# Moving the store of split weight operands from SyncE's queue to ScalarE's

## The chip, the cores and the metric

The kernel runs on one core of a Trainium2 chip. The metric is the device time of one execution in microseconds (us); several executions are given by their median. The engines are PE (TensorE, matmul), DVE (VectorE), ACT (ScalarE), POOL (GpSimd) and SP (SyncE, which here only issues DMAs). An instruction that issues a DMA waits in its engine's own program, in order, for the data and the buffers that it needs; "SPq" in the rows is such an issue on SP.

## What is computed

One layer of a residual trunk on x of 2048 tokens × 1024 channels, float32, cut to what matters (d_ff is 2816, the norms are RMS norms with gains, all mixers are causal):

```python
h = rmsnorm(x, norm_mix_g)
u_lru, u_gate, u_pool = split(h @ w_in)                # 512 columns each
xc = causal_depthwise_conv(u_lru, conv_w, conv_b)      # width 4
y_lru = rg_lru(xc, ...) * gelu(u_gate)                 # gated linear recurrence over the tokens
y_pool = pool_mixer(u_pool, ...)                       # trailing means of 2, 4, 8, 16, minus u
y = concat(rmsnorm(y_lru), rmsnorm(y_pool))
x = x + y @ w_out
h = rmsnorm(x, norm_ffn_g)
x = x + (silu(h @ ffn_w1) * (h @ ffn_w3)) @ ffn_w2
return rmsnorm(x, final_norm_g)
```

## The kernel before

Every large matmul is done on pairs: an operand is split into hi (rounded, written by an ACT copy) and lo (the rest, a subtraction on DVE or POOL), and `mm3` (L237 to L239) multiplies hi·hi, hi·lo and lo·hi into one bank of PSUM. A weight tile `w_hl` holds hi and lo of 128 × 512 weights, 512 KB; there are four such buffers (`wsp`), and six buffers of 256 KB for raw weights as they come from memory (`load_raw`, L208).

A weight is split once, at its first use. `split_kept` writes hi (L224) and lo (L234), and then stores the pair to a cache in device memory (L203). Later uses reload the finished pair from the cache with `kept` (L190, L194) and need no ACT or DVE work. There are 268 stores: 40 go to `cio_d`, the caches of the input and output projections, and 228 to `c13_d` and `c2_d`, those of the feed-forward weights.

The time falls into three stretches. From 0 to about 540 us four chunks of 512 tokens go through norm, input projection (`x_stage`, `u_stage`), the two mixers (`mixers`) and the output projection (`out_stage`); chunk 0 splits the weights, the others reload them. From 540 to 1265 us the feed-forward runs over the first half of the tokens in eleven inner steps, with a Strassen-like scheme of seven products for each block, and splits and stores its weights. From 1265 us on it runs over the second half, out of the cache, without a store of this kind.

The order of the instructions on each engine isn't written out: a scheduler sets it from a simulated timeline and from priorities (`AHEAD` 400 and `FIRST` 1500 for splits, evacuations and norms). So a change of one line can move other instructions, on other engines too.

In the mixer of chunk 0 (`mixers`), names in the order listings are: `ps_g` the gate products, `t0` and `t1` the gates' tanh (L431), `th` and `t0` again the tanh and exponential of the decay (L439, L440), `m` the input factor (L445 to L447, with a square root on ACT), the product of `t1` and `m` on POOL (L453), the scan `xc` (L455), `win` the pooling windows on POOL (L470), `pl` the pooled values (L474), and `sq` the squares (L288, L291) for the norm, whose column sums are small matmuls (L256). `x_hi` and `x_lo` (L337, L338) are the pair of the next chunk's input. In the feed-forward `f_hi`/`f_lo` is the pair of an activation, `e` and `u` are evacuations from PSUM.

Of the kernel before, what the change touches and what calls it, by code (L numbers as in the profile page):

```python
# [9 lines left out]
F32 = mybir.dt.float32  # L10
# [60 lines left out]
def trunk(ctx: ExitStack, tc: tile.TileContext, xT, w_io, w13, w2, gates, pool_w, w_inT, vecs,  # L71
          consts, outT):
    nc = tc.nc
# [103 lines left out]
    def wsp(name, shape):  # L177
        return pool.tile(list(shape), F32R, name=name, tag="wsp", bufs=N_WSP)
# [19 lines left out]
    def split_kept(src, cache, prepare=AHEAD, eng=None):  # L198

        w_ = wsp("w_hl", (P, 2, W))  # L200
        with tc.high_priority(prepare):
            split(w_[:, 0], w_[:, 1], src, eng)
        nc.sync.dma_start(cache, w_.bitcast(F32))  # L203
        return w_[:, 0], w_[:, 1]

    def load_raw(src, shape):
# [24 lines left out]
    def split(hi, lo, src, eng=None):  # L231

        copy_a(hi, src)
        (eng or nc.vector).tensor_tensor(lo, src, hi.bitcast(F32), ALU.subtract)  # L234
# [114 lines left out]
    def weights(blk):  # L349

        if blk in split_before:
            return [kept(cio_d[blk, h]) for h in range(2)]
        split_before.add(blk)
        src = wp_d[blk - 8] if 8 <= blk < 12 else w_io[blk if blk < 8 else blk - 4]
        raw = [load_raw(src[:, NB * h:NB * (h + 1)], (P, NB, P)) for h in range(2)]
        return [split_kept(raw[h].rearrange("p k m -> p (k m)"), cio_d[blk, h], FIRST, eng("w", blk))
                for h in range(2)]
# [226 lines left out]
    def ffn1(hf, j, w, ops, s, after):  # L584
# [14 lines left out]
        def product(n, ps, a, b, fresh):  # L599
            wh, wl = split_kept(b, c13_d[j, w, n]) if hf == 0 else kept(c13_d[j, w, n])  # L600
            for kk in range(NB):
                col = slice(kk * P, kk * P + P)
                mm3(ps, wh[:, col], wl[:, col], a[0][:, kk], a[1][:, kk],
                    fresh and kk == 0, kk == NB - 1, skip_group_check=True)
# [76 lines left out]
    def ffn2(hf, j, s, acc, G):  # L681
# [15 lines left out]
        def product(n, banks, a, b, fresh):  # L697
            wh, wl = split_kept(b, c2_d[j, n]) if hf == 0 else kept(c2_d[j, n])
            for dp, ps in enumerate(banks):
                col = slice(P * dp, P * (dp + 1))  # L700
                mm3(ps, wh[:, col], wl[:, col], a[0], a[1], fresh, True, skip_group_check=True)
# [260 lines left out]
```

## Time and profile before

| | before |
|---|---|
| median of 3 executions | 1935.81 us (1935.36 to 1936.9) |
| profiled execution | 1939.97 us |
| its span | 1938.2 us |
| PE busy | 1832.8 us, 95% |
| DVE busy | 1355.5 us, 70% |
| POOL busy | 928.5 us, 48% |
| ACT busy | 769.5 us, 40% |
| mean granted clock of PE | 0.977 |

The span is the profiled part of that one execution. An engine's busy time leaves out the issuing of DMAs. All views of the trace are of this one execution; the time of a change is measured against the median.

### The profile page before, as it was taken

The numbers are of one execution on the slowest core, as the hardware profiler recorded it, in microseconds if no ns is written. First come the engines' busy times: TensorE is split into PE (matmuls) and PEld (weight loads), VectorE is DVE, ScalarE is ACT, GpSimd is POOL, SyncE is SP. The second block draws the span as 40 slices with busy tenths as digits, with TensorE's granted clock in tenths as the row PEclk, the third lists the DMA queues.
The fourth block names the chain that finished last, engine by engine and source line by source line (L and its number), as shares of the span: only waits on it lengthen the run. The fifth ranks groups of instructions, "written<-read, shape, count | busy, mean of one in ns | idle before, by whom it ended". The sixth has DMA issues, their size and how long they took to land.

```text
span 1938.2 us, 23419 instructions
## 1 busy us (share of the span) xinstructions
PE 1832.8 (95%) x8016; PEld 1487.6 (77%) x8016; DVE 1355.5 (70%) x2004; ACT 769.5 (40%) x1294; POOL 928.5 (48%) x633
## 2 busy tenths in 40 slices
PE   7989999999988999999999999799999999999996
PEld 5778888787767777777777787577888888888885
DVE  7598499876669778777887878875444445444457
ACT  5463546362334444443444434442322223322223
POOL 3361723332136567666676668373333334432373
PEclk9999999999989999999999999899999999999998
DMA  9956855476987666566656666868555555555552
GB/s 322 321 206 219 323 201 179 148 288 227 394 328 260 227 246 223 217 238 220 245 210 231 230 246 230 313 206 298 186 197 194 195 187 183 201 190 195 195 174 87
DMA packets 160838, 444.69 MB, mean 229 GB/s; under 512 B 17872, under 2 KB 20048, under 8 KB 155728
## 3 DMA queue, kind: packets, MB, share of 16 engines
q1 hardware_dynamic: 160720, 443.20, 64.1%
q8 instruction: 63, 1.03, 0.2%
q14 instruction: 55, 0.45, 0.1%
HBM read 275.36 MB, written 167.77 MB: 229 GB/s over the span
## 4 chain that ended last, share of the span: by engine, by line
PE 69%; DVE 17%; issue 5%; DMA 3%; ACT 2%; POOL 2%; SPq 0%; DVEq 0%; ACTq 0%; POOLq 0%
PE ps L239 17%; PE ps L237 16%; PE ps L238 16%; DVE w_hl L234 3%; PE pV L238 2%; PE pV L239 2%; PE pV L237 2%; PE pX L237 2%; PE pX L238 2%; PE pX L239 2%; DMA c_d<-w_hl 1%; PE pY L237 1%; PE pY L238 1%; PE pY L239 1%; DVE sf L719 1%
## 5 line engine op out<-in xcount | busy, mean ns | idle before, releaser
L710 POOL TENSOR_TENSOR G<-G,e 128x512 f32<-128x512 f32 x152 | 227.8, 1516 | 132.1 <-ACT e L224 129.7
L239 PE MATMUL ps<-h_hi,w_hl 128*128 128x512 f32 x616 | 249.0, 405 | 26.2 <-DVE w_hl L234 26.0
L237 PE MATMUL ps<-h_hi,w_hl 128*128 128x512 f32 x616 | 245.5, 401 | 17.7 <-DVE u L636 10.2
L238 PE MATMUL ps<-h_lo,w_hl 128*128 128x512 f32 x616 | 244.9, 398 | 0.0
L237 PE MATMUL ps<-h_hi,w_kept 128*128 128x512 f32 x616 | 240.9, 392 | 2.0 <-DMA w_kept<-c_d 1.2
L238 PE MATMUL ps<-h_lo,w_kept 128*128 128x512 f32 x616 | 240.9, 391 | 0.0
L239 PE MATMUL ps<-h_hi,w_kept 128*128 128x512 f32 x616 | 238.8, 391 | 0.0
L291 POOL TENSOR_TENSOR sq<-sq 128x512 f32<-128x512 f32 (+1 forms) x71 | 99.7, 1407 | 167.0 <-ACT sq L288 165.6
L239 PEld LDWEIGHTS ps<-h_hi,w_hl 128*128 128x128 f32 x616 | 117.9, 191 | 65.7 <-DVE w_hl L234 40.9
L234 DVE TENSOR_TENSOR f_lo<-sf,f_hi 128x512 fp32r<-128x512 f32 x80 | 92.3, 1154 | 106.8 <-PE pZ L238 37.9
L237 PEld LDWEIGHTS ps<-h_hi,w_hl 128*128 128x128 f32 x616 | 118.0, 191 | 49.6 <-ACT w_hl L224 11.2
L710 POOL TENSOR_TENSOR acc<-acc,e 128x512 f32<-128x512 f32 x80 | 123.3, 1570 | 61.5 <-ACT e L224 60.2
L632 POOL TENSOR_TENSOR u<-u,u 128x512 f32<-128x512 f32 x44 | 66.1, 1502 | 179.2 <-DVE u L630 179.1
L706 DVE TENSOR_TENSOR acc<-pV,acc 128x512 f32<-128x512 f32 x160 | 107.9, 685 | 47.4 <-PE pV L239 46.6
L234 DVE TENSOR_TENSOR w_hl<-raw,w_hl 128x512 fp32r<-128x512 f32 x120 | 130.7, 1091 | 12.1 <-ACT w_hl L224 11.6
L238 PEld LDWEIGHTS ps<-h_lo,w_hl 128*128 128x128 f32 x616 | 118.1, 192 | 25.2
L237 PEld LDWEIGHTS ps<-h_hi,w_kept 128*128 128x128 f32 x616 | 115.8, 188 | 27.8 <-DVE acc L837 1.6
L239 PEld LDWEIGHTS ps<-h_hi,w_kept 128*128 128x128 f32 x616 | 115.7, 188 | 25.4 <-DMA w_kept<-c_d 0.3
L238 PEld LDWEIGHTS ps<-h_lo,w_kept 128*128 128x128 f32 x616 | 115.8, 188 | 25.0
L224 ACT ACTIVATE f_hi<-sf 128x512 fp32r<-128x512 f32 x80 | 50.6, 633 | 202.3 <-DVE sf L719 151.9
L224 ACT ACTIVATE w_hl<-t 128x512 fp32r<-128x512 f32 x96 | 60.3, 628 | 165.6 <-DMA c_d<-w_hl 83.2
L237 PE MATMUL ps<-x_hi,w_kept 128*128 128x512 f32 x288 | 115.0, 401 | 1.4 <-DVE u_g L388 1.4
(359 smaller groups left out, 4520.1 us busy)
## 6 DMA issues: line engine op xcount, KB each, us to landing
c_d<-w_hl SPq DMA_DIRECT2D x228, 512.0 KB, 2.9
w_kept<-c_d SPq DMA_DIRECT2D x130, 512.0 KB, 3.7
w_kept<-c_d SPq DMA_DIRECT2D x196, 256.0 KB, 3.4
w_kept<-cio_d SPq DMA_DIRECT2D x68, 512.0 KB, 3.9
raw<-w SPq DMA_DIRECT2D x132, 256.0 KB, 3.3
w_kept<-cio_d SPq DMA_DIRECT2D x104, 256.0 KB, 3.3
cio_d<-w_hl SPq DMA_DIRECT2D x40, 512.0 KB, 5.2
h_lo<-h_d SPq DMA_DIRECT2D x14, 1024.0 KB, 9.6
```

The source lines that it names most:

```text
L224: return nc.scalar.activation(out, in_, AF.Copy)
L234: (eng or nc.vector).tensor_tensor(lo, src, hi.bitcast(F32), ALU.subtract)
L237: i = nc.tensor.matmul(ps, wh, xh, start=first, stop=False, **kw)
L238: nc.tensor.matmul(ps, wh, xl, start=False, stop=False, **kw)
L239: nc.tensor.matmul(ps, wl, xh, start=False, stop=last, **kw)
L291: eng.tensor_tensor(total, total, sq, ALU.add)
L632: nc.gpsimd.tensor_tensor(u3, u3, u2, ALU.add)
L706: nc.vector.tensor_tensor(dst[dp], ps, dst[dp], ALU.add)
L710: nc.gpsimd.tensor_tensor(dst[dp], dst[dp], e, ALU.add)
L719: nc.vector.tensor_tensor(out, a, b, op)
```

## The change

The store of a split pair is issued by ACT (`nc.scalar`) where it was issued by SP (`nc.sync`). All loads, and all other stores, stay on SP.

```diff
--- before.py
+++ after.py
@@ -200,7 +200,7 @@
         w_ = wsp("w_hl", (P, 2, W))
         with tc.high_priority(prepare):
             split(w_[:, 0], w_[:, 1], src, eng)
-        nc.sync.dma_start(cache, w_.bitcast(F32))
+        nc.scalar.dma_start(cache, w_.bitcast(F32))
         return w_[:, 0], w_[:, 1]
```

Three places of the new order follow. A row has the line, the operation, out<-in, the tile's size and how many alike follow each other.

SP at the start of the program, before and then after: `x_raw` is the input of chunk 0, `raw` a raw weight, `cio_d_75<-w_hl` the store.

```order
L325 DMA x_raw_174<-xT 128x512 x3
L325 DMA x_raw_192<-xT 128x512 x3
L203 DMA cio_d_75<-w_hl_180 128x1024
L203 DMA cio_d_75<-w_hl_184 128x1024
L325 DMA x_raw_192<-xT 128x512
L208 DMA raw_302<-w_io 128x512
```

```order
L325 DMA x_raw_174<-xT 128x512 x3
L325 DMA x_raw_192<-xT 128x512 x4
L208 DMA raw_302<-w_io 128x512
L208 DMA raw_304<-w_io 128x512
L208 DMA raw_340<-w_io 128x512
```

The fourth load of x_raw_192 and the weight loads behind it stood behind two stores and now stand ahead of every store.

ACT where the mixer of chunk 0 meets the input of chunk 1, before and then after.

```order
L224 ACTIVATE w_hl_802<-raw_796 128x512
L479 ACTIVATE y_p_1058<-pl_1071,bs_70,vec_60 128x512
L337 ACTIVATE x_hi_840<-x_raw_836,vec_60 128x512 x4
L337 ACTIVATE x_hi_850<-x_raw_838,vec_60 128x512 x4
L431 ACTIVATE t0_918<-ps_g_964,hb_67 128x512
L431 ACTIVATE t1_919<-ps_g_969,hb_67 128x512
```

```order
L224 ACTIVATE w_hl_802<-raw_796 128x512
L203 DMA cio_d_75<-w_hl_798 128x1024
L479 ACTIVATE y_p_1058<-pl_1071,bs_70,vec_60 128x512
L203 DMA cio_d_75<-w_hl_802 128x1024
L431 ACTIVATE t0_918<-ps_g_964,hb_67 128x512
L431 ACTIVATE t1_919<-ps_g_969,hb_67 128x512
L439 ACTIVATE th_1002<-t0_918,sp2_170 128x512
L440 ACTIVATE t0_918<-t0_918,nsp4_172 128x512
L337 ACTIVATE x_hi_840<-x_raw_836,vec_60 128x512 x4
L337 ACTIVATE x_hi_850<-x_raw_838,vec_60 128x512 x4
```

The first gates' tanh and exponential stood behind the eight x_hi copies and now stand ahead of them. DVE in the same mixer, before and then after:

```order
L452 SCALAR_TENSOR_TENSOR t1_919<-t1_919,xc_917 128x512
L441 SCALAR_TENSOR_TENSOR t0_918<-t0_918,th_1002 128x512
L474 SCALAR_TENSOR_TENSOR pl_1097<-win_1095,u_p3_831 128x512
L477 TENSOR_TENSOR first_1099<-win_1095,cst_62 128x16
L478 TENSOR_TENSOR pl_1097<-first_1099,u_p3_831 128x16
L445 SCALAR_TENSOR_TENSOR m_1010<-t0_918 128x512
```

```order
L445 SCALAR_TENSOR_TENSOR m_1010<-t0_918 128x512
L452 SCALAR_TENSOR_TENSOR t1_919<-t1_919,xc_917 128x512
L446 TENSOR_SCALAR m_1010<-m_1010 128x512
L451 TENSOR_SCALAR t0_918<-t0_918 128x512
L441 SCALAR_TENSOR_TENSOR t0_918<-t0_918,th_1006 128x512
L474 SCALAR_TENSOR_TENSOR pl_1097<-win_1095,u_p3_831 128x512
```

The factor m_1010 stood behind the pooled values pl_1097 and now stands ahead of them; the first L452 and the L441 of th_1002 have moved further ahead, before the x_lo of the next chunk.

ACT in one step of the feed-forward, before and then after.

```order
L224 ACTIVATE w_hl_8564<-t3_8562 128x512
L224 ACTIVATE w_hl_8590<-raw_8524 128x512
L224 ACTIVATE e_8490<-pY_8458 128x512
L224 ACTIVATE e_8493<-pY_8459 128x512
L224 ACTIVATE w_hl_8620<-raw_8618 128x512
L224 ACTIVATE f_hi_8638<-s_8309 128x512
```

```order
L224 ACTIVATE w_hl_8590<-raw_8524 128x512
L203 DMA c13_d_76<-w_hl_8564 128x1024
L224 ACTIVATE e_8490<-pY_8458 128x512
L224 ACTIVATE e_8493<-pY_8459 128x512
L203 DMA c2_d_77<-w_hl_8590 128x1024
L224 ACTIVATE w_hl_8620<-raw_8618 128x512
L224 ACTIVATE f_hi_8638<-s_8309 128x512
```

The copies keep their order, and a store now stands between the evacuations e and the hi copy of the next weight, w_hl_8620.

## Rows read from the trace of the kernel before

**Rows 1.** The page, busy time of an engine.

```profile
PE 1832.8 (95%) x8016; PEld 1487.6 (77%) x8016; DVE 1355.5 (70%) x2004; ACT 769.5 (40%) x1294; POOL 928.5 (48%) x633
```

**Rows 2.** Windows: length, busy us and instructions per engine, clock, DMA share, GB/s.

```profile
0.00:100.00 100.00, 86.26 (x392) 69.93 (x393) 62.74 (x150) 52.47 (x85) 35.18 (x31) 0.97 0.91 324
...
600.00:1200.00 600.00, 571.69 (x2429) 454.63 (x2428) 491.22 (x571) 263.69 (x469) 415.69 (x261) 0.99 0.63 230
...
1300.00:1850.00 550.00, 546.90 (x2392) 449.03 (x2392) 269.30 (x362) 151.57 (x257) 196.29 (x142) 1.00 0.59 204
```

**Rows 3.** The line of the store: ns min/median/max, first and last start.

```profile
L203 SPq DMA_DIRECT2D c_d<-w_hl x228: 319/320/1511, 546.3 to 1262.6; - x114
L203 SPq DMA_DIRECT2D cio_d<-w_hl x40: 319/327/1342, 8.1 to 221.2; - x40
```

**Rows 4.** Waits of SP's queue: us in total, times, longest.

```profile
SPq L203 <- DVE w_hl L234: 455.8, 210, 6.9
```

**Rows 5.** Timeline of SP's queue at the start: start us, us.

```profile
4.01 2.54 SPq L325 DMA_DIRECT2D x_raw<-xT  x4
8.13 1.00 SPq L203 DMA_DIRECT2D cio_d<-w_hl  x2
9.18 0.86 SPq L325 DMA_DIRECT2D x_raw<-xT  x1
```

**Rows 6.** Timeline of ACT at the start, with the wait in brackets.

```profile
17.18 0.72 ACT L337 ACTIVATE x_hi<-x_raw,vec 128x512 fp32r<-128x512 f32 x1 [1.46 <-DMA x_raw<-xT]
```

**Rows 7.** Timeline of PE at the start.

```profile
17.96 0.50 PE L237 MATMUL ps<-x_hi,w_hl 128*128 128x512 f32 x1 [2.50 <-ACT x_hi L337]
```

**Rows 8.** The page, DMA queues: packets, MB, share of 16 engines.

```profile
q1 hardware_dynamic: 160720, 443.20, 64.1%
```

**Rows 9.** The chain that ended last, from 92 to 150 us: start, us.

```profile
98.21 0.73 ACT x_hi L337
...
111.52 5.09 issue
116.64 1.41 POOL t L453
...
141.56 0.43 PE ps L237
...
145.83 0.43 PE ps L238
```

**Rows 10.** Timeline of DVE from 98 to 120 us.

```profile
98.97 2.75 DVE L338 SCALAR_TENSOR_TENSOR x_lo<-x_raw,vec,x_hi 128x512 fp32r<-128x512 f32 x3 [2.27 <-ACT x_hi L337]
...
109.67 0.68 DVE L441 SCALAR_TENSOR_TENSOR t<-t,th 128x512 f32<-128x512 f32 x1
111.55 0.69 DVE L474 SCALAR_TENSOR_TENSOR pl<-win,u_p 128x512 f32<-128x512 f32 x1 [1.20 <-POOL win L470]
...
118.07 2.29 DVE L455 TENSOR_TENSOR_SCAN xc<-t,t 128x512 f32<-128x512 f32 x1 [0.59 <-POOL t L453]
```

**Rows 11.** Timeline of PE from 134 to 150 us.

```profile
139.06 1.86 PE L256 MATMUL cols<-ones,sq 128*128 128x1 f32 x8 [6.89 <-DVE sq L291]
```

**Rows 12.** Waits: us in total, times, longest us.

```profile
ACT w_hl L224 <- DMA c_d<-w_hl: 87.3, 28, 5.1
...
PE ps L239 <- DVE w_hl L234: 26.0, 23, 2.5
```

**Rows 13.** Timeline of all engines in one feed-forward step.

```profile
984.82 0.63 ACT L224 ACTIVATE w_hl<-raw 128x512 fp32r<-128x512 f32 x1
...
985.65 1.78 DVE L234 TENSOR_TENSOR w_hl<-raw,w_hl 128x512 fp32r<-128x512 f32 x1
...
988.93 0.39 PE L237 MATMUL ps<-h_hi,w_hl 128*128 128x512 f32 x1
```

## The prediction

> **What bounds the kernel now.** I read the page first: TensorE (PE) is busy 95% of the span [rows 1], so the end moves only where PE stands still or runs at a lower clock. The windows say where. From 1300 to 1850 us PE never lacks work: 2392 matmuls in 546.90 us, 0.2286 us each. By that pace the 2429 matmuls between 600 and 1200 us need 555 us of 600, so about 45 us are lost there, and the 392 in the first 100 us need 90, so 10 are lost [rows 2]. The changed line stops acting at 1262.6 us [rows 3]: the whole second half has no stores of this kind, and can only be shifted.
>
> Then the stores themselves. There are 268, each holds its queue for 0.32 us in the median and at most 1.51 us [rows 3]: 268 × 0.32 = 86 us of queue time that moves from SP to ACT. What SP does most around them is wait for their data: 455.8 us in 210 waits for the DVE subtraction [rows 4]. A store thus leaves when its lo half exists, and no queue can send it sooner. What leaves sooner is a load that now stands behind such a waiting store.
>
> **The change part by part.**
>
> *The start.* The first order fences show the fourth load of x_raw_192 behind two stores on SP. SP issues x loads until 6.55 us, waits until 8.13 us for store data, spends 1.00 us on the two stores, and starts the load at 9.18 us [rows 5]. The load's arrival ends ACT's wait at 17.18 us [rows 6], and PE's wait of 2.50 us at 17.96 us for the x_hi made from it [rows 7]. In the changed order all four loads stand ahead of everything else, so this one can leave near 6.6 us, 2.6 us earlier. The next weights (raw_302) stand right behind and move by as much, so the next PE operand moves along. I take −2.5 us. Bounds: 0, if the data path is already full (the DMA engines are 0.91 busy over the first 100 us [rows 2]) and only the order of bytes changes; −5, if PE is also spared a stretch at the lower clock like the one priced below.
>
> A rule of the Trainium skill speaks against this gain: DMA: Bandwidth & Descriptors, "Issuing engines are not separate DMA queues", says that transfers run on the same 16 engines and interleave whichever engine started them, and that several issuers save only the initiation time on the sequencer, usually small. By it the time would stay near 1935.8. The trace agrees as to the bandwidth (all of this traffic shows as one queue class, 64.1% of the engines' time [rows 8]); but here SP's wait for the store's data stands ahead of the load as well, and the rule does not count that.
>
> *The mixer of the first chunk.* The schedule moves work here, though no store is on the path. Before, ACT runs eight x_hi copies from 98.21 us, which wait for PE, ahead of the gate tanh t0_918; DVE runs pl_1097, which waits for the fourth pooling window until 111.5 us, ahead of m_1010; so POOL's product t1 starts at 116.64 us, when ACT's square root of m is there, 5.09 us after its last window ended [rows 9, 10]. At the end of this chain PE stands for 6.89 us before the column sums at 139.06 us [rows 11], and the eleven matmuls at 141.56 to 145.83 us run at 0.43 us each rather than 0.23, the lower of the clock's two levels: 11 × 0.2 = 2.2 us [rows 9]. After, tanh stands ahead of x_hi, and m_1010 ahead of pl_1097, so t1 can follow the last window at once. But these 5.09 us are not the gain, since DVE is nearly continuously busy from 98.97 to 139 us and the same work stands ahead of the sum in both orders. What it saves is its idle time: two instructions of 0.68 us (L452, L441) that move into its wait of 2.27 us before 98.97, and the waits of 1.20 and 0.59 us at 111.55 and 118.07 [rows 10]. 1.36 + 1.20 + 0.59 = 3.15; I take −3. Bounds: 0, if other waits fill in, and −5.09 − 2.2 = −7.3.
>
> *The first half of the feed-forward, 540 to 1265 us (228 stores).* Here a raw load that stood behind a store leaves up to one issue, 0.32 us, earlier. It waits for a raw buffer first, which the same lo subtraction frees, so the queue costs it no more than that. PE's stalls are mostly waits for lo halves (26.0 us in 23 waits for DVE's w_hl [rows 12]), made by DVE in order behind other DVE work. On ACT 0.32 us is added per store, while ACT is busy 263.69 of 600 us [rows 2], so the cover is ACT's idle time. But ACT works in order, and a store now holds whatever stands behind it until lo is done. The tightest place I found is in the third pair of order fences: the store of w_hl_8590 stands ahead of the hi copy of w_hl_8620. Its lo ends at 985.65 + 1.78 = 987.43 us; with 0.32 for the issue and 0.63 for the copy, hi is there at 988.38, against 984.82 + 0.63 before. PE first wants it at 988.93 [rows 13]. The margin is 0.55 us, and the next thing late is that matmul. I take 0 for the stretch. Bounds: −3.5 (one 0.32 us in each of eleven steps, reaching PE each time) and +26 (below).
>
> Other reordered work (gates of chunk 1, the turn into the feed-forward) has no stall that I can tie to the move; I take 0, ±3.
>
> The sum: −2.5 − 3 + 0 = −5.5. The profiled execution took 1939.97 us, 1938.2 of it span, and 4.2 more than the median of 1935.81, so the traced stalls may be a little large; I apply the difference to the median: 1930.3 us.
>
> **The rivals.** *No change* (chance 0.27): the loads were bound by buffers and by bandwidth, the start's 2.5 us are lost again to the next operand, and DVE stays full in the mixer. For it: DMA 0.91 busy at the start, DVE's full row. Against it: the 2.50 us wait has one releaser, that load. One of the two gains alone leaves 1933, none 1935.8; the case runs from 1932 to 1939.7. The rule of the Trainium skill cited above (DMA: Bandwidth & Descriptors, same section) puts the result here.
>
> *Slower, ACT held by its own stores* (0.21). Mechanism: in each step of the feed-forward a store holds ACT until a lo half is done, and the hi copy behind it comes after PE wants it. It decides once an issue on ACT costs over 0.32 + 0.55 = 0.87 us, or lo ends that much later in the new order. At SP's longest issue, 1.51 us, the example's hi is at 989.57, 0.64 us late. With two to four such places in each of some ten full steps that is 13 to 26 us: 1943 to 1956. For it: ACT already waits 87.3 us in 28 waits for stores to land before it may overwrite a buffer [rows 12], so a late store returns to ACT as a late buffer. Against it: the typical issue is 0.32 us.
>
> *A larger gain* (0.12, part of faster): both gains reach their bounds with the clock kept high, and loads gain in each step: −5 − 7.3 − 3.5 = −15.8, 1920.
>
> **How the numbers follow.** My forecast, with gains between 4 and 10 us, has 0.40. What a measurement of this kernel can tell from no change is 0.2%, 3.9 us: faster is below 1931.9 (0.40 + 0.12 = 0.52), same up to 1939.7 (0.27), slower above (0.21). The forecast's own range is 1926 to 1932. The range for 8 in 10 goes from 1921, which leaves out the extreme of the larger gain, to 1943, which takes in no change and the slower case up to where its worked prices begin (small misses on ACT, and reorderings at +3, lie between 1939.7 and 1943).
>
> **What would show it.** Right: the fourth load of x_raw_192 issued near 7 us and no wait of 2.5 us on PE near 18 us; t1 on POOL right behind the fourth window, and the wait before the column sums shorter by about 3 us; the same 45 us lost between 600 and 1200 us. Wrong: PE waiting for ACT's w_hl (not DVE's) in every step; stores on ACT lasting near 1 us; or the start's transfers landing no earlier than before.

## The result and the profile after

The changed kernel takes 1958.01 us in the median (1956.21 to 1960.4), the kernel before beside it 1936.36: ratio 1.0113, 95% interval [1.0095, 1.013]. I had forecast 1930.3 us, between 1921 and 1943. It is slower, and 15 us above the upper end of the range. Two of the runs below had one execution each far above the others at a lower granted clock (2264.59 and 3028.12 us); their ratios leave these out, their medians do not.

The windows of the changed kernel, columns as in [rows 2]:

```profile
0.00:100.00 100.00, 88.14 (x411) 70.99 (x412) 68.07 (x156) 59.02 (x94) 34.88 (x31) 1.00 0.91 327
...
600.00:1200.00 600.00, 550.63 (x2333) 437.61 (x2334) 469.33 (x547) 251.38 (x449) 374.86 (x248) 0.99 0.61 220
...
1300.00:1850.00 550.00, 546.42 (x2395) 449.30 (x2394) 275.06 (x371) 149.50 (x254) 202.83 (x147) 0.99 0.60 204
```

Against [rows 2], the first 100 us hold 411 matmuls where they held 392, so the start is ahead. From 600 to 1200 us there are 2333 where there were 2429: 96 × 0.2286 = 22 us lost within this window. From 1300 us on nothing differs. A count of PE's instructions in the trace, from zero, says when the n-th one starts, and makes the place exact:

```
n-th PE instruction   before us   after us   lead
 200                     57.94      55.37    -2.57
 600                    156.84     152.47    -4.37
1400                    332.03     328.99    -3.04
1600                    382.83     374.14    -8.69
2600                    630.69     617.67   -13.01
5400                   1333.02    1349.30   +16.27
8000                   1915.99    1932.23   +16.24
```

In these two executions the stretch up to the feed-forward gained 13 us, more than I had hoped for, and the feed-forward lost 29. Each column is one execution: that of the kernel before took 3.6 us more than the median given here and that of the changed kernel 1.8 less, so a gain in this table can be some us too large and a loss too small. The stores of the feed-forward in the changed kernel, and ACT's waits (us in total, times, longest):

```profile
L203 ACTq DMA_DIRECT2D c_d<-w_hl x228: 326/327/389, 535.9 to 1270.5; - x114
```

```profile
ACT u L224 <- DVE w_hl L234: 41.9, 16, 3.0
...
ACT w_hl L224 <- DVE w_hl L234: 23.8, 23, 1.6
...
ACT e L224 <- DVE w_hl L234: 17.8, 20, 2.7
```

Issuing on ACT costs 0.33 us, as on SP [rows 3]. But ACT now waits 83.5 us in 59 waits for DVE's lo halves, with a store in front of the work named; in the kernel before such a wait shows once, with 2.8 us. That looks like my slower rival, ACT held by its stores. The experiments had to say whether it is.

One step of the feed-forward after the change, PE, then DVE, then POOL, from the timeline (start us, us):

```profile
1045.26 0.50 PE L237 MATMUL ps<-h_hi,w_hl 128*128 128x512 f32 x1 [1.33 <-DVE u L636]
...
1059.25 0.50 PE L239 MATMUL ps<-h_hi,w_hl 128*128 128x512 f32 x1 [2.61 <-DVE w_hl L234]
```

```profile
1044.51 0.69 DVE L636 TENSOR_TENSOR u<-ps,u 128x512 f32<-128x512 f32 x1 [2.42 <-POOL u L632]
```

```profile
1041.62 1.62 POOL L596 TENSOR_TENSOR t__9190<-raw,t 128x512 f32<-128x512 f32 x1
1043.21 1.27 POOL L632 TENSOR_TENSOR u<-u,u 128x512 f32<-128x512 f32 x1
```

PE waits 1.33 us for a sum u3 (L636), which waits for POOL's addition (L632), which stands behind a weight combination t2_ of 1.62 us. Later in the step it waits 2.61 us for a lo half. No store stands in this chain on DVE or POOL: what has changed there is the order. In the program's order, POOL and then DVE, before (-) and after (+):

```
-L632 TENSOR_TENSOR u3_8882<-u3_8882,u2_8858 128x512
 L596 TENSOR_TENSOR t2__9190<-raw_9084,t1_9188 128x512
+L632 TENSOR_TENSOR u3_8882<-u3_8882,u2_8858 128x512

-L670 TENSOR_TENSOR c_8944<-ps_8839,u2_8858 128x512
 L234 TENSOR_TENSOR w_hl_9032<-raw_9030,w_hl_9032 128x512
+L670 TENSOR_TENSOR c_8944<-ps_8839,u2_8858 128x512
 L671 TENSOR_TENSOR s_8743<-s_8743,c_8944 128x512
```

Over the whole run PE's waits for lo halves have grown from 26.0 us [rows 12] and those for this sum from 11.0 us; the first row is of the kernel before, the other two of the changed one:

```profile
PE ps L237 <- DVE u L636: 11.0, 3, 7.9
```

```profile
PE ps L239 <- DVE w_hl L234: 41.1, 35, 2.9
PE ps L237 <- DVE u L636: 21.6, 12, 8.0
```

So three theories stood: **hold** (ACT waits in order for lo halves), **order** (the schedule planned the engines' work anew for the new queue), and **queues** (a second DMA queue, with the issue on ACT).

### The profile page after: what moved, and what is told of

The parts are those of the page before. It is cut to its first block, busy times and chain, and to the rows that moved or that the text cites. A ratio compares the mean times of both kernels' runs of the same rounds, so it can differ in the third digit from the quotient of the medians.

```text
span 1954.4 us, 23367 instructions
## 1 busy us (share of the span) xinstructions
PE 1828.6 (94%) x8016; PEld 1480.6 (76%) x8016; DVE 1357.5 (69%) x2004; ACT 767.5 (39%) x1294; POOL 916.5 (47%) x633
## 4 chain that ended last, share of the span: by engine, by line
PE 60%; DVE 20%; POOL 7%; issue 6%; DMA 4%; ACT 2%; SPq 0%; ACTq 0%; DVEq 0%; POOLq 0%
PE ps L239 15%; PE ps L237 14%; PE ps L238 14%; DVE w_hl L234 4%; DVE f_lo L234 2%; POOL t L596 2%; DMA raw<-w 2%; PE pX L239 1%; PE pX L237 1%; PE pX L238 1%; PE pV L238 1%; PE pV L239 1%; PE pV L237 1%; DVE xc L417 1%; PE pY L237 1%
## 5 line engine op out<-in xcount | busy, mean ns | idle before, releaser
L710 POOL TENSOR_TENSOR G<-G,e 128x512 f32<-128x512 f32 x152 | 223.5, 1488 | 113.8 <-ACT e L224 113.8
L234 DVE TENSOR_TENSOR w_hl<-raw,w_hl 128x512 fp32r<-128x512 f32 x120 | 126.5, 1055 | 30.6 <-ACT w_hl L224 25.1
L632 POOL TENSOR_TENSOR u<-u,u 128x512 f32<-128x512 f32 x44 | 64.0, 1455 | 177.7 <-DVE u L630 177.7
L596 POOL TENSOR_TENSOR t<-raw 128x512 f32<-128x512 f32 x44 | 71.0, 1616 | 107.8 <-DVE w_hl L234 50.1
```

Of the source, the lines that this page charges most:

```text
L596: nc.gpsimd.tensor_tensor(t, a, b, ALU.subtract)
L632: nc.gpsimd.tensor_tensor(u3, u3, u2, ALU.add)
L710: nc.gpsimd.tensor_tensor(dst[dp], dst[dp], e, ALU.add)
```

## The experiments

**Halves of the change.** The store gets its queue as an argument (its default is SP or ACT, and the call for the projections names the other): only the projections' 40 stores on ACT, or only the feed-forward's 228.

```diff
-    def split_kept(src, cache, prepare=AHEAD, eng=None):
+    def split_kept(src, cache, prepare=AHEAD, eng=None, q=nc.sync):
...
-        nc.sync.dma_start(cache, w_.bitcast(F32))
+        q.dma_start(cache, w_.bitcast(F32))
```

> Only the 40 stores of the projection weights (cio_d) go to ACT, the 228 of the feed-forward stay on SP. The changed kernel is 13 us ahead of the kernel before at its 2600th matmul (617.67 against 630.69 us) and 16 us behind at the end, so it lost 29 us in the feed-forward. All theories (ACT held by its stores; POOL's new order; two DMA queues that share the engines) put the loss with the feed-forward's stores. Then the time is 1936 - 11 to - 13 = 1923 to 1925 us. If instead the feed-forward loses because of what comes out of the mixers, it stays near 1950.

> The opposite half: the 228 feed-forward stores on ACT, the 40 projection stores on SP. If gain and loss are separate, the loss stands alone: 1936 + 26 to 29 = 1962 to 1965 us. If the loss is less, say 1950, the two halves act on each other.

Measured 1930.97 us (ratio 0.9966 [0.9952, 0.998]) and 1969.04 us (1.0163 [1.0146, 1.018]). Gain and loss are separate, and each stands with its own stores: 7 us gained, 31 lost. Against the kernel before beside them, 1937.91 us, the gain is 4 us smaller and the loss 2 us larger than the ranges that I had taken from the table of single executions.

**Stores later, and POOL's order.** First each feed-forward store is issued behind the hi copy of the next weight; then, instead, POOL's u3 is kept ahead of t2_; then both. From the edits, against the changed kernel:

```diff
-        nc.scalar.dma_start(cache, w_.bitcast(F32))
+        if eng:
+            nc.scalar.dma_start(cache, w_.bitcast(F32))
+        else:
+            store_pending(hi)
+            pending.append((cache, w_))
```

```diff
+            if name == "t2_" and "u3" in last:
+                issue_after(i, last["u3"])
```

> The feed-forward store of a weight is issued on ACT only after the hi copy of the next weight, so that copy is no longer held by it. POOL's order keeps t2_ ahead of u3 as in the changed kernel, and the number of stores and queues is the same. Theory hold (ACT waits in order for lo halves; 87.5 us of ACT's waits are for DVE's lo halves against 2.8 before): most of the 29 us comes back, 1933 to 1942 us. Theory order (POOL's t2_ ahead of u3 makes PE wait for DVE's u): some 14 us stay, 1945 to 1952 us. Theory queues (loads and stores share the DMA engines and land later): no change, 1955 to 1960 us.

> The change, with POOL's add into u3 made to stand ahead of the next weight combination t2_, as it stood before the change. Stores stay on ACT as in the changed kernel. Theory order: PE's waits for DVE's u (22 us in ten waits against 8 in one) go and 10 to 14 us come back, 1944 to 1948 us. Theory hold: the hi copies are as late as they were, at most a few us come back, 1952 to 1958 us. Theory queues: 1955 to 1960 us.

> Both mends at once: the feed-forward store behind the hi copy of the next weight, and POOL's u3 ahead of t2_. Stores later alone gave 1941.1 us, u3 first alone 1948.4, the change 1958. If hold and order are two separate losses, both go and the time is that of the variant with only the projection stores on ACT, 1929 to 1934 us. If the order only mattered through the hold, it stays near 1941, 1938 to 1943 us.

Measured 1941.13 us (1.002 [1.0006, 1.0035]), 1948.43 us (1.0062 [1.0045, 1.008]) and 1943.96 us (1.0036 [1.0022, 1.0051]). Each mend brings back 10 to 17 us, and they don't add up: with both the time is above either of the ranges I had given. But with each edit the schedule planned everything anew: with both edits DVE's order within a step is again that of the kernel before. So these runs can't tell hold from order, though by what was expected of it the first looked like a proof of hold.

**Holding ACT without a DMA.** Stores stay on SP. In the place that each store has in the changed kernel, ACT reads one column of the lo half; a second version reads 176 columns. The heart of the edit:

```diff
+                    i = nc.scalar.activation(small("touch", 1), waiting.pop(0)[:, 1, 0:1].bitcast(F32),
+                                             AF.Copy)
+                issue_after(i, hi)
```

> All stores back on SP, as in the kernel before. In the place of each of the 228 feed-forward stores ACT runs a copy of one column of the lo half, in the place among the hi copies that the store has in the changed kernel (in 144 of 228 ahead of the next hi copy). So ACT waits for every lo half, and no DMA is issued from ACT. Theory hold: the feed-forward loses 20 to 30 us, 1955 to 1967 us. Theory queues (a second queue of DMAs, issue cost on ACT): within a few us of the kernel before, 1935 to 1941 us.

> As the kernel in which ACT reads one column of every lo half in the place of the store (1935.6 us, no loss), but it reads 176 columns, so that ACT is busy for about as long as with the issue of a store, 0.33 us, rather than 0.20. The queue alone, with the old order, cost 9 us. If that is ACT's issue time, 1941 to 1947 us; if it is what the second queue does to landings, 1934 to 1938 us.

Measured 1935.55 us (0.9992 [0.998, 1.0004]) and 1938.96 us (1.0006 [0.9995, 1.0016]). The waits of the first of them, of ACT and then of PE:

```profile
ACT touch L211 <- DVE w_hl L250: 166.3, 138, 3.2
```

```profile
PE ps L256 <- DVE w_hl L250: 30.3, 29, 2.5
```

ACT was held for 166.3 us, twice as long as in the changed kernel, and PE's wait for lo halves is 30.3 us against 26.0 before [rows 12]. So holding ACT for every lo half is not enough for the loss. The wider read took 0.347 us each, about as long as the issue of a store, and cost nothing either. In both, DVE and POOL ran the feed-forward in the order of the kernel before. The schedule was planned with the reads in it, so this does not say what a hold costs in an order that was not planned for it.

**Order and queue, crossed.** The order in which PE, DVE, ACT and POOL run their instructions is taken from one of the two programs and imposed on the other, by a chain of edges that set the issue order alone.

```diff
+    for steps in ISSUE.values():
+        n, ahead = 0, None
+        for step in steps.split():
+            n += int(step)
+            if ahead:
+                tc.add_manual_dep(nc.get_inst_by_name(f"I-{n}"), ahead, mybir.DependencyInfo(
+                    mybir.DependencyClass.NoSync, mybir.DependencyReason.DATA), reason="issue order")
+            ahead = f"I-{n}"
```

> All stores on SP as before the change, but PE, DVE, ACT and POOL run their 11733 computing instructions in exactly the order that they have in the changed kernel. Holding ACT for every lo half without a DMA cost nothing, so the theory hold has fallen; two are left. Theory order: the loss lies in the order that the schedule planned for the new queue, and comes with it: 1950 to 1962 us. Theory queues (what issuing and landing from ACT's queue does, together with the places of the stores on ACT): the order alone costs little, 1924 to 1938 us.

> All stores on ACT as in the changed kernel, but PE, DVE, ACT and POOL run their computing instructions in exactly the order of the kernel before; a store stands ahead of the next hi copy in 137 of 228 places (144 in the changed kernel). Theory order: no loss in the feed-forward, 1931 to 1940 us. Theory queues: the loss stays though the order is the old one, 1950 to 1968 us. Both in part: between.

Measured 1959.01 us (1.0103 [1.0086, 1.012]) for the new order with the stores on SP, and 1947.87 us (1.005 [1.0033, 1.0066]) for the old order with the stores on ACT. The first is the time of the changed kernel to 1 us, with all stores on SP. Its windows row, ACT's wait and PE's waits:

```profile
600.00:1200.00 600.00, 556.41 (x2317) 441.59 (x2318) 478.79 (x546) 247.78 (x446) 379.69 (x247) 0.97 0.60 219
```

```profile
ACT w_hl L224 <- DVE w_hl L234: 2.9, 1, 2.9
```

```profile
PE ps L239 <- DVE w_hl L234: 37.8, 24, 2.9
...
PE ps L237 <- DVE u L636: 16.5, 9, 8.0
```

ACT waits for a lo half once, 2.9 us, and still 2317 matmuls fit where 2429 did. SP's order was left free, but its loads in the feed-forward stand as before. So the new order alone is enough for a loss of this size. It is not made in quite the same way: of the 600 us PE stands idle for 43.6 here and for 49.4 in the changed kernel, against 28.3 before, and the granted clock is 0.97 here and 0.99 in the other two. In the changed kernel hi copies also come late, as DVE's wait for them says; here it is 48.1 us in 38 waits, before 39.2 in 36:

```profile
DVE w_hl L234 <- ACT w_hl L224: 63.2, 81, 4.5
```

How much of the changed kernel's own loss passes through these late copies was not parted. The second run shows that the queue, or the places of the stores on it, can cost something with the old order: 9 us.

**Which engine's order.** Stores on SP; only POOL's order in the feed-forward is the new one, or only that of DVE and ACT (these two were not parted, and PE's order there was left to the schedule, which planned most of the new one).

> Stores on SP, and the computing order of the kernel before on PE, DVE and ACT; only POOL runs the feed-forward in the order of the changed kernel (t2_ ahead of u3 among others). The whole order cost 20 us with stores on SP. If POOL's part is what makes PE wait for DVE's u, 10 to 14 us, so 1947 to 1953 us; if the loss lies with DVE and ACT, under 5 us, 1934 to 1943 us.

> The other part: stores on SP, POOL in the order of the kernel before, DVE and ACT in the feed-forward in the order of the changed kernel (hi copies of raw weights and of activations ahead of evacuations, lo halves ahead of the sums), PE's order there left to the schedule. If the loss lies here, 12 to 20 us, 1949 to 1958 us; if it lies with POOL, under 5 us, 1934 to 1943 us.

Measured 1944.77 us (1.004 [1.0025, 1.0055]) and 1961.94 us (1.0125 [1.011, 1.014]). POOL's order, where I had looked first, costs 6 us, between the two ranges given; that of DVE and ACT, with the order of PE that was planned for it, costs 23 us, which is 4 above its range. Together they make 29 us, about what the whole order loses in the feed-forward: the 20 us by which it is slower, and the 7 that it gains in the mixers, as the runs on the mixers will show.

**Where the 9 us of the queue are.** Stores on ACT, the old order, and each feed-forward store behind the next hi copy.

> All stores on ACT, computing order of the kernel before on PE, DVE, ACT and POOL, and each feed-forward store behind the hi copy of the next weight. With the stores at their free places this order took 1947.9 us, 9 over the kernel before. ACT's busy time and its waits for lo halves cost nothing with the DMAs on SP. If the 9 us need the store ahead of the next hi copy, 1934 to 1941 us; if they come from what the second queue does to landings wherever the store stands, 1944 to 1950 us.

Measured 1933.6 us (0.9975 [0.9959, 0.9991]): not 9 us slower but 5 faster; where the 5 come from was not followed up. The queue itself is no cost here; a store on it ahead of the next hi copy is. DVE's wait for hi copies tells it, first with the stores at their free places, then with the later ones:

```profile
DVE w_hl L234 <- ACT w_hl L224: 64.6, 76, 4.3
```

```profile
DVE w_hl L247 <- ACT w_hl L237: 43.1, 36, 5.2
```

In the kernel before, this wait is 39.2 us in 36 waits, so with the stores at their free places some 40 more hi copies came late. With the reads of one column in like places it was 44.8 us in 50. Why they did less stays open; their schedule was planned with them, while this order was imposed.

**The gain in the mixers.** Only the first weight block's two stores on ACT; only the other 38; and all on SP with the new order up to the first feed-forward weight.

> Only the two stores of the first weight block go to ACT; the fourth load of x_raw_192 then stands ahead of all stores. If the start is worth the 2.5 us that the wait at 17.96 us showed, PE is 2 to 3 us ahead at its 200th matmul and the time is 1933 to 1936 us by this chip's 1937.9 for the kernel before, less what later reordering takes back.

> The other 38 projection stores go to ACT, the first two stay on SP. If the start gives 2.5 us of the 7 that all 40 gave, the rest gives 4 to 5: 1933 us, with no lead at the 200th matmul and a lead between the 1400th and the 1600th, where the column sums at 367.70 us wait. If the lead at the 1600th matmul hangs on the start, this shows no change, 1936 to 1939 us.

> Stores on SP. Up to the first feed-forward weight the computing order of the changed kernel, from there that of the kernel before. If the lead that the changed kernel has after the mixers is the order's as well (7.5 us with the order alone at the 2200th matmul, 2.2 us with the queue alone), the time is 1929 to 1932 us, as good as with the projection stores on ACT.

Measured 1935.39 us (0.9997 [0.9986, 1.0008]), 1930.88 us (0.9963 [0.995, 0.9976]) and 1931.17 us (0.9965 [0.9952, 0.9978]). The first block's stores alone give nothing in the end, though PE is 2.4 us ahead at its 200th instruction. The second run gave the whole gain of the 40 stores, and against what I had expected PE was 2.3 us ahead at its 200th instruction there too, though the fourth load of x_raw_192 still left behind two stores. The 7 us come with the new order, and also with the stores on SP.

**What the runs point to.** The mixers' new order, the feed-forward's old one, all stores on ACT, those of the feed-forward later.

> What the runs point to, in one kernel: all stores on ACT, each feed-forward store behind the hi copy of the next weight, the changed kernel's computing order up to the first feed-forward weight and the old order from there. The mixers' order gave 7 us with stores on SP, the later stores with the old order 4 to 5. If they add up, 1925 to 1929 us by 1938 for the kernel before; if the lead does not carry over, 1931 to 1934 us.

Measured 1927.91 us (0.994 [0.9926, 0.9953]): 10 us faster than before, 30 faster than the change.

## Why the prediction was wrong

**The step that failed** is the feed-forward's "I take 0 for the stretch", with bounds of −3.5 and +26: it measured +29 in the traces and 31 by the medians of the run with these stores alone. I walked one place of the new order through on ACT, with the times of DVE and POOL as they had been, and put the rest under "Other reordered work ... I take 0, ±3". But DVE's and POOL's orders had changed in every step too, and ACT's in part: the hi copy of a combined weight passed that of an activation. The new orders alone are enough for the loss: 1959.01 us with the stores where they were.

**The slower rival** named the stretch and a price of the right size (13 to 26 us, chance 0.21), and a mechanism that is not the main one; that its times of 1943 to 1956 us lie near the measured one is in good part luck. It was to decide once an issue on ACT cost over 0.87 us, or lo ended that much later in the new order. The issue costs 0.33. Its sign, PE waiting for ACT's w_hl in every step, did not show (11.6 us in 7 waits, 13.4 in 9 before). Lo does come later (41.1 us of PE's waits against 26.0), but it does so with no store on ACT too (37.8). Held for 166.3 us, ACT lost nothing. A store's place ahead of the next hi copy does cost 9 us with the old order; that is the part of the rival that is left.

**The start**, −2.5 us. PE was 2.57 us ahead at its 200th instruction. The x loads now leave in one piece, until 7.37 us, and no wait of 2.5 us is left at 18 us:

```profile
4.02 3.35 SPq L325 DMA_DIRECT2D x_raw<-xT  x5
```

```profile
18.57 0.51 PE L239 MATMUL ps<-x_hi,w_hl 128*128 128x512 f32 x1 [0.61 <-POOL w_hl L234]
```

How much of the lead is this load's, one trace can't say: with the load still behind two stores the kernel with the other 38 stores on ACT was 2.26 us ahead there, and with it ahead of them the old order with all stores on ACT 0.28. Over the traces of all 18 kernels, the nine with the load ahead lead at the 50th instruction by 2.9 us in the mean (1.9 to 3.5), the other nine by 0.5 (from 1.0 behind to 1.8 ahead). So mechanism and size were about right for the stretch; that the gain reaches the end was not: alone, it changed nothing that could be measured.

**The mixer of the first chunk**, −3 us, measured about zero: from the 400th instruction (at 101.86 us before and 97.64 after) to the 600th, the stretch with the column sums, the lead grew by 0.1 us. POOL's product did move up, from 116.64 us [rows 9] to 110.34, but the column sums still wait for a full DVE:

```profile
110.34 1.35 POOL L453 TENSOR_TENSOR t<-t,m 128x512 f32<-128x512 f32 x1 [2.84 <-ACT m L447]
```

```profile
135.20 1.87 PE L256 MATMUL cols<-ones,sq 128*128 128x1 f32 x8 [7.93 <-DVE sq L291]
```

The wait is 7.93 us against 6.89 [rows 11]. It ended 3.9 us earlier, and PE was 4.2 us ahead already when it came to it. The three waits of DVE that I had added up are gone, and it idles 2 us less in the 42 before the sums; that this does not reach PE was the term's lower bound, though not for the reason given there.

**The unforeseen gain** lies between the 1400th and the 1600th instruction, 5.65 us. Before, PE waited there 1.37 us for DVE's u_g (L388) and 2.98 us for the squares of the column sums, and then ran about twelve matmuls at 0.43 us each, the lower of the two clock levels; after, one wait of 2.25 us is left, and the matmuls behind it keep 0.23 us. The column sums, before and then after:

```profile
367.70 1.49 PE L256 MATMUL cols<-ones,sq 128*128 128x1 f32 x8 [2.98 <-DVE sq L291]
```

```profile
362.23 1.02 PE L256 MATMUL cols<-ones,sq 128*128 128x1 f32 x8 [2.25 <-DVE sq L291]
```

This gain is no chance of one execution: these 200 instructions take 50.3 to 50.8 us in the nine traces with the mixers' old order, or nearly that, and 45.1 to 46.8 in the nine with the new one, with the stores on either queue. The window of 60 us around it, in the kernel before and then in the changed one (the column behind POOL is the granted clock):

```profile
330.00:390.00 60.00, 55.65 (x243) 45.67 (x242) 50.98 (x103) 22.20 (x34) 15.98 (x12) 0.94 0.45 151
```

```profile
320.00:380.00 60.00, 57.75 (x267) 47.96 (x266) 53.59 (x106) 27.88 (x40) 19.62 (x14) 1.00 0.48 167
```

**The no-change rival** had a rule behind it (the Trainium skill, DMA: Bandwidth & Descriptors, "Issuing engines are not separate DMA queues"). The one queue class of [rows 8] could not bear on it, since one engine issued everything there. The changed kernel fits the rule: the stores on ACT show as a queue class of their own, but the feed-forward's raw loads and its stores land no sooner for it; they took 3.7 and 3.6 us where they took 3.3 and 2.9. The small gain that the rule allows fits the run with the first block's two stores alone (0.9997). The rule does not speak of the loss: with the order alone, all on one queue and with landings of 3.3 and 2.9 us, an equal one came.

## What to carry to other kernels

Where a scheduler sets the order, a change of queue is a change of the whole program: read the new order on every engine of the stretch that bounds, step by step, and price each instruction that has passed another, before the queue itself. Compare leads in traces with the medians: here one execution was 3.6 us off. To find a cause, impose the old order on the new program and the new order on the old one; an edit that makes the scheduler plan anew mends or hurts by its own plan and proves little. A store on a computing engine is best tried behind the next work of that engine that others wait for: here this turned a loss of 9 us into a gain of 5.

## What I had not expected of the hardware

Two programs that differ in the order of their computing instructions alone take 1959.01 us and, beside it, 1938.57: 1% for the same work, queues and data. And ACT has room for 268 issues of 0.33 us each, 88 us in all, in a kernel that is 5 us faster than the one before (1933.6 against 1938.24 us).
